# The S5 matrix to the state made row-major from transposed factors, with SyncE carrying its loads

## The chip, the core and the metric

The kernel runs on one NeuronCore of a Trainium2 chip. The core has five engines with an instruction queue each: TensorE (PE in the profile; its weight loads are PEld), VectorE (DVE), ScalarE (ACT), GpSimd (POOL) and SyncE (SP), which here only issues DMAs. The DMAs of all queues share 16 DMA engines. An engine runs its queue in order: where an instruction waits for a semaphore, all behind it wait too. The metric is the device time in microseconds.

## The reference, cut to what matters

One step of a hybrid diffusion backbone: two layers, each a SwiGLU feed-forward half, a mixer and a second feed-forward half, on 128 context and 256 latent tokens of width 1024. One branch of the mixer is a bidirectional diagonal state-space layer (S5) with 32 groups of 16 channels and 64 complex states for each direction:

```python
abar_r, abar_i = mag * jnp.cos(a_im * dt), mag * jnp.sin(a_im * dt)
...
bbar_r = qr[..., None] * b_re - qi[..., None] * b_im
bbar_i = qr[..., None] * b_im + qi[..., None] * b_re
bu_r = jnp.einsum('gph,blgh->blgp', bbar_r, u)
bu_i = jnp.einsum('gph,blgh->blgp', bbar_i, u)
...
_, _, sr, si = lax.associative_scan(_ssm_combine, (ar, ai, bu_r, bu_i), reverse=reverse, axis=1)
y = jnp.einsum('ghp,blgp->blgh', c_re, sr) - jnp.einsum('ghp,blgp->blgh', c_im, si)
```

The kernel works the scan in chunks of 8 tokens. Three tables for each group hold what a chunk needs: the *matrix to the state* (`ms`: a power of `abar` times `bbar`, for each of 8 positions and 16 channels), the *matrix from the state* (`my`: a power times `c`), and the *responses* inside a chunk (`k_d`, gathered to `mi`). They depend on weights alone.

## The kernel before

TensorE runs in an order written by hand; the orders of the other four engines come from a scheduler that places each instruction by its priority and by the time at which it reckons the operands to be there.

**Weights.** All projections stream weights in *units* of 128 x 1024 values (512 KB): SyncE loads `wr` (L149), ACT copies it to the rounded `wh` (L126), VectorE makes the rest `wl` (L105, called as `sub`), and TensorE runs `mm3`, three matmuls for each of 8 tiles of a unit: `wh` by the high half of the input (L198), `wh` by the low half (L199) and `wl` by the high half (L200). `wr`, `wh` and `wl` have three buffers each, and a unit is prepared two units ahead (`LOOK = 2`). The names in the trace are `mm<-hh,wh` and the like, by input.

**Side work.** Everything that isn't a projection is a generator, called a track; at each unit the running tracks are advanced by some steps, a step ending at a `yield`. `tables(0)` runs as a track beside the first feed-forward half of layer 0, `tables(1)` beside the first half of layer 1, both with the loads of the modulation weights (`modw` on SyncE, L374, then 8 matmuls each, L386).

**The tables.** `s5_tables(l)` (L924) goes over four blocks `gb` of 8 groups. For each block it transposes `cr` into `cT`, makes `bb` (the discretised `bbar`, states along the partitions, by `cmul`) and its spread-out copy `bp` (four ACT copies, L968 and L969), and loads the raw inputs of the next block (`load_bc`, on GpSimd's queue). Then come two sub-blocks `sb` of four groups. Each has six VectorE products and sums of 128 x 512 for `my`, six more for `mt` (the matrix to the state, states along the partitions), the matmuls of the responses (L1024, L1034), and eight transposes of `mt` on TensorE (in the helper `transpose`, L138), whose results ACT copies to `ms` (L1050, two of 128 x 512) before GpSimd's queue writes `ms` to DRAM. The powers of `abar` are expanded once in `s5_params` and read back as `pxl` tiles.

Of the kernel before, what the change touches and what calls it, by code (L numbers as in the profile page):

```python
# [11 lines left out]
F32 = mybir.dt.float32  # L12
# [44 lines left out]
def hybrid_step(ctx: ExitStack, tc: tile.TileContext, I, pos_r, pos_c, y_prompt, y_sample, new_state):  # L57
# [43 lines left out]
    def s1(shape, name):  # L101
        return sp.tile(shape, F32, tag="s1", name=name, bufs=7)
# [616 lines left out]
    px_d = [drm.tile([P, 2, 2, TC, G], F32, tag=f"px{l}", name=f"px{l}") for l in range(DEPTH)]  # L719
# [68 lines left out]
    def s5_params(raw, ldt):  # L788
# [81 lines left out]
        lo_i = slice(TC - 1, None, -1), slice(1, TC + 1)  # L870
        hi_i = slice(0, TC), slice(TC, 0, -1)
        for w in range(2):
            px = c4([P, DEPTH, 2, TC, G], "px")
            for i in range(2):
                for rows, ix in ((LO, lo_i[w]), (HI, hi_i[w])):
                    src = pw[rows, i, ix, :].rearrange("p n (l g) -> p l n g", l=DEPTH)
                    for l in range(DEPTH):
                        act.activation(px[rows, l, i], src[:, l], AF.Copy)
            for l in range(DEPTH):
                q.dma_start(px_d[l][:, w], px[:, l])  # L880
# [43 lines left out]
    def s5_tables(l):  # L924
        q = nc.gpsimd
        px = []
        for w in range(2):
            t = c2([P, 2, TC, G], "pxl")
            q.dma_start(t, px_d[l][:, w])
            px.append(t)  # L930
        psx, pyx = px
# [18 lines left out]
        for gb in range(G // GB):  # L950
# [9 lines left out]
            pool.memset(bb, 0.0)  # L960
# [5 lines left out]
            pool.memset(bp, 0.0)  # L966
# [4 lines left out]
            ts_(nci, cT[:, 1], -1.0)  # L971
            if gb + 1 < G // GB:
                nxt = load_bc(gb + 1)
            kall = s1([P, 2, 9 * H], "kall")
            for sb in range(GB // GS):
                s0 = sb * GS

                def pexp(tab, i):
                    v = tab[:, i, :, g0 + s0 : g0 + s0 + GS]
# [6 lines left out]
                b_r, b_i = vec(bb[:, 0]), vec(bb[:, 1])  # L986
                my = c4([P, GS, 2, TC, H], "my")
                t1, t2 = c2(sh, "tp1"), c2(sh, "tp2")
# [864 lines left out]
```

## Time and profile before

| | |
|---|---|
| median of 3 runs | 1775.85 us (1775.21 to 1778.99) |
| profiled execution, own time | 1775.03 us |
| its span | 1773.0 us |
| mean granted clock of TensorE | 0.997 |
| TensorE busy | 1743.7 us (98% of the span) |
| VectorE busy | 1246.8 us (70%) |
| ACT busy | 795.8 us (45%) |
| moved by DMA | 344.48 MB, mean 194 GB/s |

The profile is one execution. The busy time of an engine is summed over its instructions; matmuls overlap their neighbours, so a main matmul of 0.34 us is followed by the next after about 0.17 us. A line of a timeline gives start, duration, engine, line, operation, tiles, shapes and count, and in square brackets the idle time of the engine before it with what ended it. All VectorE products have the line of the helper, L105, so they are told apart by their tiles. The span leaves out some 2 us around it.

### The profile page before, as it was taken

The numbers are of one execution on the slowest core, as the hardware profiler recorded it, in microseconds if no ns is written. First come the engines' busy times: TensorE is split into PE (matmuls) and PEld (weight loads), VectorE is DVE, ScalarE is ACT, GpSimd is POOL, SyncE is SP. The second block draws the span as 40 slices with busy tenths as digits, with TensorE's granted clock in tenths as the row PEclk, the third lists the DMA queues.
The fourth block names the chain that finished last, engine by engine and source line by source line (L and its number), as shares of the span: only waits on it lengthen the run. The fifth ranks groups of instructions, "written<-read, shape, count | busy, mean of one in ns | idle before, by whom it ended". The sixth has DMA issues, their size and how long they took to land.

```text
span 1773.0 us, 30946 instructions
## 1 busy us (share of the span) xinstructions
PE 1743.7 (98%) x12116; PEld 1652.8 (93%) x12116; DVE 1246.8 (70%) x2344; ACT 795.8 (45%) x1330; POOL 203.5 (11%) x400
## 2 busy tenths in 40 slices
PE   7999999999999999999999999999999999999997
PEld 4899999999999989999999899999999999999997
DVE  5496676778986885678487666767799788544435
ACT  3344333575355553233366233336744546423233
POOL 2012343310010000000001133232100000000000
PEclk9999999999999999999999999999999999999999
DMA  9778788776753677788346776667666443444332
GB/s 343 249 224 275 231 252 269 226 198 190 240 157 108 186 238 228 237 280 257 112 131 208 234 224 215 175 195 233 162 210 200 131 123 116 132 130 127 123 125 77
DMA packets 253753, 344.48 MB, mean 194 GB/s; under 512 B 22399, under 2 KB 216651, under 8 KB 253608
## 3 DMA queue, kind: packets, MB, share of 16 engines
q1 hardware_dynamic: 228504, 299.18, 53.4%
q0 software_dynamic: 17088, 39.51, 7.5%
q10 hardware_dynamic: 8016, 3.82, 0.8%
q8 instruction: 95, 1.56, 0.4%
q14 instruction: 50, 0.41, 0.1%
HBM read 309.75 MB, written 32.70 MB: 193 GB/s over the span
## 4 chain that ended last, share of the span: by engine, by line
PE 81%; DVE 10%; ACT 4%; DMA 3%; issue 2%; SPq 0%; ACTq 0%; DVEq 0%
PE mm L198 25%; PE mm L200 25%; PE mm L199 25%; PE ax L386 3%; DVE wl L105 3%; DVE cacc L123 2%; DMA wr<-in_w_gate_dram 1%; DVE m_t L105 1%; PE tb L138 1%; ACT wh L126 1%; DVE m_hh L105 1%; DMA modw<-in_w_mod_dram 1%; DVE macc L123 1%; DMA wr<-in_w_in_dram 1%; ACT zp L1125 0%
## 5 line engine op out<-in xcount | busy, mean ns | idle before, releaser
L105 DVE TENSOR_TENSOR wl<-wr,wh 128x1024 fp32r<-128x1024 f32 (+2 forms) x389 | 457.0, 1175 | 352.1 <-ACT wh L126 347.4
L126 ACT ACTIVATE wh<-wr 128x1024 fp32r<-128x1024 f32 (+1 forms) x387 | 395.9, 1023 | 613.9 <-PE mm L199 443.9
L198 PE MATMUL mm<-hh,wh 128*128 128x384 f32 x1840 | 625.3, 340 | 2.7 <-ACT hh L621 2.7
L200 PE MATMUL mm<-hh,wl 128*128 128x384 f32 x1840 | 617.1, 335 | 4.4 <-DVE wl L105 4.2
L199 PE MATMUL mm<-hl,wh 128*128 128x384 f32 x1840 | 616.3, 335 | 0.5 <-DVE hl L105 0.3
L198 PEld LDWEIGHTS mm<-hh,wh 128*128 128x128 f32 x1840 | 345.9, 188 | 31.7 <-issue 18.1
L200 PEld LDWEIGHTS mm<-hh,wl 128*128 128x128 f32 x1840 | 345.8, 188 | 6.7 <-DVE wl L105 6.7
L199 PEld LDWEIGHTS mm<-hl,wh 128*128 128x128 f32 x1840 | 345.9, 188 | 1.2 <-DVE hl L105 1.1
L198 PE MATMUL mm<-ah,wh 128*128 128x384 f32 x800 | 273.2, 342 | 0.0
L199 PE MATMUL mm<-al,wh 128*128 128x384 f32 x800 | 269.4, 337 | 0.8 <-DVE al L105 0.8
L200 PE MATMUL mm<-ah,wl 128*128 128x384 f32 x800 | 270.0, 338 | 0.0
L198 PEld LDWEIGHTS mm<-ah,wh 128*128 128x128 f32 x800 | 150.2, 188 | 10.2 <-issue 6.7
L199 PEld LDWEIGHTS mm<-al,wh 128*128 128x128 f32 x800 | 150.4, 188 | 1.7 <-DVE al L105 1.1
L200 PEld LDWEIGHTS mm<-ah,wl 128*128 128x128 f32 x800 | 150.2, 188 | 0.0
L123 DVE SCALAR_TENSOR_TENSOR x<-mm,gt,x 128x128 f32<-128x128 f32 x224 | 83.1, 411 | 33.3 <-PE mm L200 33.1
L198 PE MATMUL mm<-xh,wh 128*128 128x386 f32 x240 | 84.7, 353 | 0.0
L126 ACT ACTIVATE ah<-av 128x384 fp32r<-128x384 f32 x82 | 42.1, 519 | 89.4 <-DVE av L105 89.1
L200 PE MATMUL mm<-xh,wl 128*128 128x386 f32 x240 | 81.9, 341 | 0.0
L199 PE MATMUL mm<-xl,wh 128*128 128x386 f32 x240 | 81.9, 341 | 0.0
L123 DVE SCALAR_TENSOR_TENSOR macc<-modw,silu_c,macc 128x1024 f32<-128x1024 f32 x56 | 69.9, 1278 | 14.9 <-DMA modw<-in_w_mod_dram 14.9
L123 DVE SCALAR_TENSOR_TENSOR cacc<-pad,pv,cacc 128x399 f32<-128x399 f32 x120 | 69.7, 627 | 0.0
L386 PE MATMUL ax<-modw,silu_c 128*32 128x512 f32 (+1 forms) x576 | 63.2, 511 | 0.7 <-DMA modw<-in_w_mod_dram 0.7
(316 smaller groups left out, 1820.0 us busy)
## 6 DMA issues: line engine op xcount, KB each, us to landing
wr<-in_ffn_w_dram SPq DMA_DIRECT2D x256, 512.0 KB, 3.6
modw<-in_w_mod_dram SPq DMA_DIRECT2D x144, 512.0 KB, 5.4
wr<-in_w_gate_dram SPq DMA_DIRECT2D x48, 512.0 KB, 3.8
wr<-in_w_in_dram SPq DMA_DIRECT2D x24, 512.0 KB, 3.6
my<-my POOLq DMA_DIRECT2D x16, 512.0 KB, 5.5
ms<-ms POOLq DMA_DIRECT2D x16, 512.0 KB, 4.9
m_ms<-ms SPq DMA_DIRECT2D x16, 512.0 KB
m_my<-my SPq DMA_DIRECT2D x16, 512.0 KB, 7.4
```

The lines of the kernel that those rows point to most:

```text
L105: (eng or dve).tensor_tensor(out, a, b, op=op)
L123: dve.scalar_tensor_tensor(out, a, s, b, op0=op0, op1=op1)
L126: act.activation(hi, full, AF.Copy)
L138: pe.transpose(out, in_, ident[:rows, :rows])
L198: pe.matmul(out, wh[:, k, cols], xh, start=first, stop=False)
L199: pe.matmul(out, wh[:, k, cols], xl, start=False, stop=False)
L200: pe.matmul(out, wl[:, k, cols], xh, start=False, stop=last)
L386: pe.matmul(b[32 * s : 32 * s + 32, :w], silu_c[:, k, :], raws[i][:, c : c + w], start=(k == 0), stop=(k == KD - 1), skip_group_check=True,)
```

## The change

The matrix to the state is made with the 128 chunk rows (position and channel) along the partitions, the layout in which it is needed, so that its transposes go. What is transposed instead are its factors. `s5_params` transposes the powers once (eight transposes, tile `pws`) and writes them to DRAM as `pt_d`. For each block, `factor_rows` transposes a copy `bc` of `bb` (two transposes), ACT copies the result to `bts`, and eight DMAs on GpSimd's queue write it to `btr_d`. For each sub-block `to_rows_in` loads `pt` (eight DMAs of 64 KB on SyncE, one for each position, each read 16 times over for the 16 channels) and `bt` (one of 512 KB on GpSimd's queue), and `to_rows` makes `ms` of them in six VectorE operations of 128 x 512. `load_bc` moves from GpSimd's queue to SyncE's: eight DMAs of 32 KB for each block. The fills of `bb` and `bp` move from GpSimd to VectorE, for the halves that need them, and the tag `s1` gets nine buffers in place of seven. The steps of a block are in another order: `my` of both sub-blocks first, with `factor_rows` and the responses between their steps, then `to_rows` of both.

```diff
-        return sp.tile(shape, F32, tag="s1", name=name, bufs=7)
+        return sp.tile(shape, F32, tag="s1", name=name, bufs=9)
...
+        pws = c4([P, TC, P], "pws")
+        for i in range(2):
+            b = tb_bank()
+            for m in range(TC // 2):
+                transpose(
+                    b[:, m * P : (m + 1) * P], pw[:, i, 2 * m : 2 * m + 2, :].rearrange("p n r -> p (n r)"), P
+                )
+            bv = b.rearrange("p (m s) -> p m s", s=P)
+            o = pws[:, 4 * i : 4 * i + 4]
+            act.activation(o[:, ::-1, LO], bv[:, :, LO], AF.Copy)
+            act.activation(o[:, :, HI], bv[:, :, HI], AF.Copy)
+            yield
...
-                    q.dma_start(braw[d * PS : (d + 1) * PS, i], I[nm][l, d, gs].rearrange("g p h -> p g h"))
+                    nc.sync.dma_start(braw[d * PS : (d + 1) * PS, i], I[nm][l, d, gs].rearrange("g p h -> p g h"))
...
-                    q.dma_start(cr[:, i, d, :], I[nm][l, d, gs].rearrange("g h p -> (g h) p"))
+                    nc.sync.dma_start(cr[:, i, d, :], I[nm][l, d, gs].rearrange("g h p -> (g h) p"))
...
-            pool.memset(bb, 0.0)
+            dve.memset(bb[:, :, :, H:], 0.0)
...
-            pool.memset(bp, 0.0)
+            dve.memset(bp[LO, :, :, H:], 0.0)
+            dve.memset(bp[HI, :, :, :H], 0.0)
...
+            bc = s1([P, 2, GB, H], "bc")
+            act.activation(bc, bb[:, :, :, :H], AF.Copy)
             if gb + 1 < G // GB:
                 nxt = load_bc(gb + 1)
+
+            def factor_rows():
+                b = tb_bank()
+                for i in range(2):
+                    transpose(b[:, i * P : (i + 1) * P], bc[:, i].rearrange("p g h -> p (g h)"), P)
+                bts = s1([P, 2, P], "bts")
+                act.activation(bts.rearrange("p i s -> p (i s)"), b[:, : 2 * P], AF.Copy)
+                for j in range(TC):
+                    q.dma_start(btr_d[l][j, :, gs].rearrange("h g x -> g h x"), bts.rearrange("r i s -> r (i s)"))
...
-                mt = c4([P, GS, 2, TC, H], "mt")
-                t1, t2 = c2(sh, "tp1"), c2(sh, "tp2")
-                mul(t1, pexp(psx, 0), b_r)
-                mul(t2, pexp(psx, 1), b_i)
+
+            def to_rows_in(sb):
+                gr = slice(g0 + sb * GS, g0 + (sb + 1) * GS)
+                pt = c4([P, 2, GS, P], "pt")
+                for j in range(TC):
+                    nc.sync.dma_start(pt[j * H : (j + 1) * H], pt_d[l][:, j, gr].unsqueeze(0).to_broadcast([H, 2, GS, P]))
+                bt = c4([P, GS, 2 * P], "bt")
+                q.dma_start(bt, btr_d[l].rearrange("j h g x -> (j h) g x")[:, gr])
...
+            def to_rows(sb):
+                pt, bt = ins[sb]
+                ms = c4([P, GS, 2, P], "ms")
+                t1, t2 = (c2([P, GS, P], f"tp{i}") for i in (1, 2))
+                mul(t1, pt[:, 0], bt[:, :, 0])
+                mul(t2, pt[:, 1], bt[:, :, 1])
                 yield
...
-                ms = c4([P, GS, 2, P], "ms")
-                for g2 in range(0, GS, 2):
-                    b = tb_bank()
-                    for j in range(4):
-                        transpose(
-                            b[:, j * P : (j + 1) * P], mt[:, g2 + j // 2, j % 2].rearrange("p i h -> p (i h)"), P
-                        )
-                    act.activation(ms[:, g2 : g2 + 2].rearrange("p g r c -> p (g r c)"), b, AF.Copy)
-                q.dma_start(ms_d[l][:, g0 + s0 : g0 + s0 + GS], ms)
+
+            mys, ins = [], []
+            yield
+            for n, _ in enumerate(from_rows(0)):
+                if n == 1:
+                    factor_rows()
+                yield
+            for n, _ in enumerate(from_rows(1)):
+                if n == 0:
+                    responses(0)
+                yield
+            to_rows_in(0)
+            yield
+            responses(1)
+            yield
+            to_rows_in(1)
+            yield from to_rows(0)
+            yield from to_rows(1)
```

The rows of the order below are of layer 0, around the start of the third block. The numbers behind the names are the tiles' own; the units that matter are, in the kernel after, `wr_2791`/`wl_2794`, then those of `wl_2837`, of `wr_2945` and `wr_3003`/`wl_3006`, one behind the other, and later `wr_3151`.

TensorE before, at the end of a unit in a sub-block's middle (`my_2904` and `mt_2946` are the two matrices of the sub-block):

```order
L200 MATMUL mm_3036<-hh3_373,wl_2960 128x384
L1024 MATMUL tb_3067<-my_2904,bp_2885 32x128 x8
L1034 MATMUL tb_3067<-cT_2868,bb_2873 32x16 x4
L1034 MATMUL tb_3067<-nci_2891,bb_2873 32x16 x4
L138 MATMUL tb_3086<-ident_92,mt_2946 128x128 x4
L138 MATMUL tb_3092<-ident_92,mt_2946 128x128 x4
L198 MATMUL mm_3035<-hh4_519,wh_2995 128x384
```

TensorE after, at the end of the unit `wl_2794`; `bc_2932` is the copy of `bb_2911`, with which the third block begins:

```order
L199 MATMUL mm_2833<-al_2631,wh_2793 128x384
L200 MATMUL mm_2833<-ah_2630,wl_2794 128x384
L138 MATMUL tb_2984<-ident_92,bc_2932 128x128 x2
L198 MATMUL mm_3001<-ah_1931,wh_2836 128x384
L199 MATMUL mm_3001<-al_1932,wh_2836 128x384
L200 MATMUL mm_3001<-ah_1931,wl_2837 128x384
```

The eight transposes of `mt` no longer stand between two units; two transposes of `bc` stand between others, at an earlier place of the block.

VectorE before, around the `wl` that goes before the first `mt` sum (`pxl_1471` is the expanded power):

```order
L105 TENSOR_TENSOR tp2_2911<-pxl_1473,cT_2868 128x512
L105 TENSOR_TENSOR tp1_2947<-pxl_1471,bb_2873 128x512
L123 SCALAR_TENSOR_TENSOR my_2904<-tp1_2910,tp2_2911 128x4x128
L123 SCALAR_TENSOR_TENSOR x5_106<-mm_2817,gt00_118,x5_106 128x256
L105 TENSOR_TENSOR tp2_2948<-pxl_1471,bb_2873 128x512
L105 TENSOR_TENSOR wl_2996<-wr_2993,wh_2995 128x1024
L105 TENSOR_TENSOR mt_2946<-tp1_2947,tp2_2948 128x4x128
L105 TENSOR_TENSOR tp1_2988<-pxl_1471,bb_2873 128x512
```

VectorE after, from `wl_3006`, the unit three behind `wl_2794` (`pt_2725` and `bt_2734` belong to the last sub-block of the block before):

```order
L105 TENSOR_TENSOR wl_3006<-wr_3003,wh_3005 128x1024
L105 TENSOR_TENSOR tp1_2787<-pt_2725,bt_2734 128x512
L105 TENSOR_TENSOR tp2_2788<-pt_2725,bt_2734 128x512
L105 TENSOR_TENSOR tp1_2822<-pt_2725,bt_2734 128x512
L105 TENSOR_TENSOR ms_2786<-tp1_2787,tp2_2788 128x4x128
L105 TENSOR_TENSOR tp2_2823<-pt_2725,bt_2734 128x512
L977 MEMSET bb_2911 128x16x16
L105 TENSOR_TENSOR ms_2786<-tp1_2822,tp2_2823 128x4x128
L105 TENSOR_TENSOR bb_2911<-cm1_2913,cm2_2914 128x8x16
L105 TENSOR_TENSOR bb_2911<-cm1_2918,cm2_2919 128x8x16
L983 MEMSET bp_2923 64x16x16
L984 MEMSET bp_2923 64x16x16
```

The six operations of `ms_2786` now follow `wl_3006` in one run, and `bb_2911` of the next block stands behind them.

SyncE before, over five units and two loads of modulation weights:

```order
L149 DMA wr_2957<-in_ffn_w1_dram 128x4x256
L149 DMA wr_2993<-in_ffn_w1_dram 128x4x256
L374 DMA modw_3134<-in_w_mod_dram 128x1024
L374 DMA modw_3136<-in_w_mod_dram 128x1024
L149 DMA wr_3037<-in_ffn_w1_dram 128x4x256
L149 DMA wr_3104<-in_ffn_w1_dram 128x4x256
L149 DMA wr_3155<-in_ffn_w1_dram 128x4x256
```

SyncE after, over the units from `wr_3003` to `wr_3151`:

```order
L149 DMA wr_3003<-in_ffn_w1_dram 128x4x256
L1043 DMA pt_2725<-pt0_142 16x2x512 x2
L149 DMA wr_3059<-in_ffn_w1_dram 128x4x256
L374 DMA modw_3181<-in_w_mod_dram 128x1024
L374 DMA modw_3183<-in_w_mod_dram 128x1024
L149 DMA wr_3107<-in_ffn_w1_dram 128x4x256
L1043 DMA pt_2725<-pt0_142 16x2x512 x2
L149 DMA wr_3151<-in_ffn_w1_dram 128x4x256
L1043 DMA pt_2725<-pt0_142 16x2x512 x3
```

The chunks of `pt_2725` now stand between the loads of units, the last three behind `wr_3151`, and the loads of the next block's inputs behind these.

## Rows read from the trace of the kernel before

**Rows 1.** The page, first lines: span; busy time of each engine, share, count.
```profile
span 1773.0 us, 30946 instructions
...
PE 1743.7 (98%) x12116; PEld 1652.8 (93%) x12116; DVE 1246.8 (70%) x2344; ACT 795.8 (45%) x1330; POOL 203.5 (11%) x400
```

**Rows 2.** Waits of TensorE: line, releaser, us in total, times, longest.
```profile
PE ax L138 <- DMA crow<-in_c_dram: 5.3, 1, 5.3
PE mm L200 <- DVE wl L105: 4.2, 5, 1.4
```

**Rows 3.** Windows: us, busy of PE, PEld, DVE, ACT, POOL, clock, DMA share, GB/s.
```profile
264.00:308.00 44.00, 44.00 (x323) 39.94 (x316) 29.61 (x48) 16.20 (x27) 15.70 (x31) 1.00 0.86 278
```

**Rows 4.** Timeline of TensorE, table stage: start, us, engine, line, tiles, count.
```profile
248.66 0.34 PE L199 MATMUL mm<-al,wh 128*128 128x384 f32 x1
...
250.54 0.44 PE L138 MATMUL tb<-ident,cr 128*128 128x128 f32 x2
250.73 0.42 PE L198 MATMUL mm<-ah,wh 128*128 128x384 f32 x1
```

**Rows 5.** Timeline of ACT at the same place.
```profile
249.04 1.06 ACT L126 ACTIVATE wh<-wr 128x1024 fp32r<-128x1024 f32 x1 [3.42 <-PE mm L199]
251.01 0.39 ACT L958 ACTIVATE cT<-tb 128x256 f32<-128x256 f32 x1 [0.92 <-PE tb L138]
252.33 0.31 ACT L968 ACTIVATE bp<-bb 64x128 f32<-64x128 f32 x1 [0.94 <-DVE bb L105]
```

**Rows 6.** Timeline of VectorE at the same place.
```profile
250.13 1.23 DVE L105 TENSOR_TENSOR wl<-wr,wh 128x1024 fp32r<-128x1024 f32 x1
...
252.52 0.28 DVE L105 TENSOR_TENSOR bb<-cm,cm 128x128 f32<-128x128 f32 x1
252.72 1.89 DVE L105 TENSOR_TENSOR tp<-pxl,cT 128x512 f32<-128x512 f32 x3
...
260.36 1.23 DVE L105 TENSOR_TENSOR wl<-wr,wh 128x1024 fp32r<-128x1024 f32 x1 [0.17 <-ACT wh L126]
261.50 0.68 DVE L105 TENSOR_TENSOR mt<-tp,tp 128x512 f32<-128x512 f32 x1
```

**Rows 7.** Timeline of the issues on SyncE at the same place.
```profile
250.63 0.82 SPq L374 DMA_DIRECT2D modw<-in_w_mod_dram  x2
251.58 10.41 SPq L149 DMA_DIRECT2D wr<-in_ffn_w_dram  x3
```

**Rows 8.** The chain of waits: start, us, engine, tile, line, count.
```profile
179.78 1.17 PE tb L138 x8
...
269.60 1.12 PE tb L138 x8
...
1198.59 1.17 PE tb L138 x8
```

**Rows 9.** TensorE by line and form: busy us, mean ns, idle before.
```profile
L138 PE MATMUL tb<-ident,mt 128*128 128x128 f32 x128 | 19.3, 287 | 0.0
```

**Rows 10.** Issues of DMAs: count, KB each, median us to landing.
```profile
mib<-kd POOLq DMA_DIRECT2D x64, 64.0 KB, 5.6
...
wr<-in_ffn_w_dram SPq DMA_DIRECT2D x16, 256.0 KB, 2.8
...
m_rho<-rhod SPq DMA_DIRECT2D x8, 200.0 KB, 8.6
```

**Rows 11.** Timeline of TensorE around 360 us, and a window of it.
```profile
360.61 0.37 PE L468 MATMUL ax<-ones,sqacc 128*32 128x1 f32 x24 [1.96 <-DVE sqacc L105]
...
362.26 0.53 PE L200 MATMUL mm<-xh,wl 128*128 128x386 f32 x1
...
360.00:365.00 5.00, 4.39 (x38) 4.38 (x39) 4.96 (x14) 1.54 (x3) 0.00 (x0) 0.66 0.91 305
```

**Rows 12.** Waits of SyncE: line, releaser, us in total, times, longest.
```profile
SPq L149 <- DVE wl L105: 1088.7, 322, 8.0
```

More of the change, by code (lines that the diff above doesn't have):

```diff
@@ L718, in hybrid_step @@
     rho_d = [drm.tile([P, 4, G // 4, NE], F32, tag=f"rhod{l}", name=f"rhod{l}") for l in range(DEPTH)]
-    px_d = [drm.tile([P, 2, 2, TC, G], F32, tag=f"px{l}", name=f"px{l}") for l in range(DEPTH)]
+    px_d = [drm.tile([P, 2, TC, G], F32, tag=f"px{l}", name=f"px{l}") for l in range(DEPTH)]
+    pt_d = [drm.tile([2, TC, G, P], F32, tag=f"pt{l}", name=f"pt{l}") for l in range(DEPTH)]
+    btr_d = [drm.tile([TC, H, G, 2 * P], F32, tag=f"btr{l}", name=f"btr{l}") for l in range(DEPTH)]
     NG = DEPTH * G
@@ L868, in s5_params @@
             yield
[L870 to L878, printed above, removed]
-            for l in range(DEPTH):
-                q.dma_start(px_d[l][:, w], px[:, l])
+        px = c4([P, DEPTH, 2, TC, G], "px")
+        for i in range(2):
+            for rows, ix in ((LO, slice(1, TC + 1)), (HI, slice(TC, 0, -1))):
+                src = pw[rows, i, ix, :].rearrange("p n (l g) -> p l n g", l=DEPTH)
+                for l in range(DEPTH):
+                    act.activation(px[rows, l, i], src[:, l], AF.Copy)
+        for l in range(DEPTH):
+            q.dma_start(px_d[l], px[:, l])
+        yield
[11 more added lines that the diff above has]
+            yield
+        for n2 in range(2):
+            for l in range(DEPTH):
+                r = n2 * NG + l * G
+                rows_d = pt_d[l].rearrange("i j g s -> (i j) g s")
+                for half, off in ((LO, 1 - n2), (HI, n2)):
+                    q.dma_start(
+                        rows_d[off::2, :, half].rearrange("m g s -> g m s"), pws[r : r + G, :, half]
+                    )
         yield
@@ L925, in s5_tables @@
         q = nc.gpsimd
[L926 to L931, printed above, removed]
+        pyx = c2([P, 2, TC, G], "pxl")
+        q.dma_start(pyx, px_d[l])
         def load_bc(gb):
@@ L993, in s5_tables @@
                 t1, t2 = c2(sh, "tp1"), c2(sh, "tp2")
[L994 removed]
+                mul(t1, pexp(1), c_r)
                 yield
[L996 removed]
+                mul(t2, pexp(0), c_i)
                 stt(
@@ L1006, in s5_tables, with responses @@
                 yield
-                mt = c4([P, GS, 2, TC, H], "mt")
-                t1, t2 = c2(sh, "tp1"), c2(sh, "tp2")
-                mul(t1, pexp(psx, 0), b_r)
-                mul(t2, pexp(psx, 1), b_i)
+            def to_rows_in(sb):
[5 more added lines that the diff above has]
+                q.dma_start(bt, btr_d[l].rearrange("j h g x -> (j h) g x")[:, gr])
+                bt = bt.rearrange("p g (i s) -> p g i s", s=P)
+                ins.append((pt, bt))
+            def to_rows(sb):
[4 more added lines that the diff above has]
+                mul(t2, pt[:, 1], bt[:, :, 1])
                 yield
-                sub(mt[:, :, 0], t1, t2)
-                t1, t2 = c2(sh, "tp1"), c2(sh, "tp2")
-                mul(t1, pexp(psx, 0), b_i)
+                sub(ms[:, :, 0], t1, t2)
+                t1, t2 = (c2([P, GS, P], f"tp{i}") for i in (1, 2))
+                mul(t1, pt[:, 0], bt[:, :, 1])
                 yield
-                mul(t2, pexp(psx, 1), b_r)
-                add(mt[:, :, 1], t1, t2)
-                for _ in range(3):
-                    yield
+                mul(t2, pt[:, 1], bt[:, :, 0])
+                add(ms[:, :, 1], t1, t2)
+                q.dma_start(ms_d[l][:, g0 + sb * GS : g0 + (sb + 1) * GS], ms)
+                yield
+            def responses(sb):
+                s0 = sb * GS
+                my = mys[sb]
                 b = tb_bank()
```

17 lines of the change are left out of this document (9 added, 8 removed).

## The prediction

> **What bounds the kernel now.** Read the page's first part first: TensorE is busy for 1743.7 of 1773.0 us [rows 1]. Next come the waits of TensorE: the longest single one is 5.3 us, at the start, and the low halves of the weights (`wl`) cost it 4.2 us in all [rows 2]. In the middle of the stage that the change rewrites it is busy for 44.00 of 44.00 us at a granted clock of 1.00, with the DMA engines at 0.86 [rows 3]. So a matmul taken off TensorE comes off the time almost whole, and a wait put on TensorE goes on whole: it runs in one written order, has nothing else to do, and no later slack gives it back.
>
> Then read how a weight unit passes from engine to engine; the rest rests on it. The last L199 of a unit started at 248.66 and ran 0.34 us [rows 4], so its `wh` buffer came free at 249.0 = E. ACT, which had waited 3.42 us for that, made the new `wh` in 1.06 [rows 5]; VectorE made `wl` of it in 1.23, ending at 251.36 [rows 6]; SyncE issued the next `wr` into the freed raw buffer at 251.58 [rows 7]. With three buffers each, that `wl` belongs to the unit three further on and that `wr` to the one six further on. So VectorE can't pass the `wl` of unit u+3 before E(u) + 2.3 us, nor SyncE the `wr` of u+6 before E(u) + 2.6.
>
> The kernel before lives with this because TensorE uses what lies behind such a `wl` only about two units later: the `mt` product that follows the `wl` of 260.36 ran at 261.50 [rows 6], and TensorE's transposes that need it came at 269.60 [rows 8].
>
> **The change: what leaves TensorE.** The 128 transposes of `mt` stand in the chain as 16 groups of 8, at 1.09 to 1.17 us, of which three are shown [rows 8]: 16 x 1.12 = 17.9 us. They are on the path, since TensorE stands still nowhere around them [rows 3]; their 32 evictions leave ACT, which was not the bound. By the Trainium skill ("TensorE: Matmul & The Clock Gate", Part 4: PE-mode transpose) a transpose took about 275 ns in one kernel's context, so that 128 would be an estimated 35 us; the rows have 287 ns for one as well [rows 9], but eight of them overlap into 1.12 us, and the rows decide.
>
> What comes instead: 8 pairs of factor transposes, bounded by the pair of `cr`, which moved the next main matmul by 0.19 us and lengthened it by 0.08 [rows 4], so 8 x 0.3 = 2.4; and 8 transposes of the powers, once, like one group, 1.1. Net for TensorE: 17.9 - 3.5 = **-14 us**.
>
> **The change: what now waits.** Nothing before shows the new order's waits; they follow from the three excerpts of the order. After unit `wl_2794` TensorE's very next instruction is now the transpose of `bc_2932`. That needs ACT's copies of `bb` (four to `bp`, one to `bc`), these need VectorE's two `bb` differences, and these stand on VectorE behind `wl_3006`, the unit three further on, and behind the six operations of `ms_2786`, which need all of `pt_2725`. The last three of its eight chunks stand on SyncE behind `wr_3151`, six further on. TensorE therefore waits for a relay that only its own last matmul sets off. Its price here, from E:
>
> - `wh` and `wl`: 2.3 us, as above; the `wr` can be issued at 2.6.
> - SyncE issues one `wr` and three chunks at 0.41 each (two took 0.82 [rows 7]), to 4.2; the last lands later by something not shown for this shape. Nearest are 2.8 for a weight of 256 KB and 5.6 for `mib`, 64 KB written by small rows [rows 10]; the chunks are 64 KB in rows of 2 KB, so I take 3.6, nearer the weights: 7.8. The short end is nothing (the chunk has landed by 2.3), the long one 8.6, that of the `m_rho` load [rows 10].
> - VectorE: six operations of 128x512 at 0.63 (three took 1.89 [rows 6]) = 3.8, the fill of `bb` about 0.3 (as its 0.28 subtractions, a guess from the nearest row) and two differences at 0.28 = 4.7: 12.5.
> - ACT: four copies at 0.31 and one like `cT` at 0.39 [rows 5] = 1.6: **14 us**.
>
> The same chain stands at the start of the second, third and fourth group block of both layers, with different covers (the first blocks have no `to_rows` ahead of them). In layer 0 the three places have chunks behind the `wr`: about 14.5, 14 and 14. In layer 1 the first has five chunks behind it: 14. The second's chunks stand behind an older `wr` and have landed: 2.3 + 4.7 + 1.6 = 8.6. The third has its `wl` out of the way; left are the last products, differences and copies, about 5, and 2 more for the `my` product that `responses` wants one unit later: 7. Sum: 14.5 + 14 + 14 + 14 + 8.6 + 7 = **+72 us**. With the chunks landed in time everywhere it is 4 x 8.6 + 8.6 + 7 = 50; with landings of 5.6 it is 80, with 8.6 it is 92.
>
> **The clock.** The trace has one idle TensorE of such a kind: 1.96 us before 360.61. A main matmul at 362.26 then took 0.53 us where its like take 0.34 [rows 4], and the slice 360 to 365 has a granted clock of 0.66 [rows 11], so the engine fell from 2.4 to 1.2 GHz for a part of it. (1 - 0.66) x 5 = 1.7 us lost. Six longer stalls: 6 x 1.7 = **+10 us**, from none (if the fall lies inside the stall) to twice that.
>
> **What I cost at nothing.** 24 MB more of transfers (128 chunks of 64 KB, 16 `bt` of 512 KB, 64 writes of factor rows of 128 KB) beside what fills 0.86 of the DMA engines in this stage [rows 3]: while TensorE stands, the queues drain, so they lose no weights of their own. The stage moved 278 GB/s, and 305 in the slice with the clock's fall [rows 3, 11], so there is a little room above. The eight loads of `b` and `c` a block on SyncE: 8 x 0.4 us of issue, hidden by the two units of weights ahead, but they add to the head of each queue they stand in. The fills on VectorE: 0.3 us each, on the chain at six places and counted there. The evictions of `pws` and of the factor rows go to ACT, in the place of 32 longer ones.
>
> **Sum.** The profiled execution took 1775.0 us (0.8 below the median of 1775.85, its span 2.0 below it). 1775 - 14 + 72 + 10 = **1843 us**.
>
> **Rivals.** *Hidden.* The queue a load is issued from makes no difference, and the waits fold into slack. The Trainium skill ("DMA: Bandwidth & Descriptors", Issuing engines are not separate DMA queues) says that spreading issues over engines saves only the sequencer's time, usually small; read so, gathering them on SyncE would cost next to nothing. As a mechanism here: SyncE's chunks would be out before TensorE reaches the end of the unit, and VectorE's differences too; 1775 - 14 = **1761**. It would need VectorE to run past `wl` of unit u+3 before E(u); ACT's 3.42 us of waiting for L199 [rows 5] speaks against it, and three `wr` issues that took 10.41 us [rows 7], with SyncE's 322 waits for `wl` of 1088.7 us in all [rows 12], show that what is long is the wait at the queue's head, not the issue. Chance 0.06, with 0.02 more for a case in which a single place waits and takes the 14 us back (about 1775).
> *Lump alone.* The chunks are always there in time and the clock recovers inside the stall: 1775 - 14 + 50 = **1811**, or 1797 if the two lesser places of layer 1 are hidden too. Chance 0.12.
> *Slower still.* Landings like `m_rho`'s, in a stage whose DMA engines are nearly full, and the clock's fall doubled: 1775 - 14 + 92 + 20 = **1873**. Chance 0.10 for over 1868.
> Where it turns: each place costs 8.6 us even with its chunks landed, so two places outweigh the 14 us; faster needs five of the six to be hidden.
>
> **How the numbers follow.** Forecast 0.70 (1815 to 1868, itself at 1843), lump alone 0.12 (1797 to 1815), slower still 0.10, hidden 0.06, even 0.02. The range goes from 1797 to 1873. A measurement here can tell about 0.2% (3.6 us). Faster 0.06, same 0.02, slower 0.92.
>
> **What would show it.** TensorE's waits in the new trace name ACT's `bc` (L991) at six places, 5 to 15 us each, right after a unit's last matmul and with `tb<-ident,bc` behind; ahead of it VectorE waits for a DMA of `pt`; the granted clock is down in the slices behind. `tb<-ident,mt` is gone, with pairs of `bc` in its place at about 0.3 us each. The forecast is wrong if these transposes find `bc` done, if their waits name the landing of the factor rows or of `cr` instead, or if TensorE waits for `wl` or `wr` all through the stage.

## The result and the profile after

The changed kernel takes 1851.34 us (median; 1848.57 to 1851.52) beside 1775.72 us for the kernel before on the same chip: a ratio of 1.0427, 95% interval 1.0411 to 1.0444. It is slower by 75.6 us. The forecast was 1843 us, slower, with a range of 1797 to 1873; its mechanism is the one that the trace shows.

The page and the waits of TensorE in the kernel after answer [rows 1] and [rows 2]. First the page (span; busy time of each engine, its share, its instructions):

```profile
span 1846.8 us, 31022 instructions
...
PE 1740.1 (94%) x12012; PEld 1648.8 (89%) x12012; DVE 1252.9 (68%) x2368; ACT 783.2 (42%) x1310; POOL 206.0 (11%) x404
```

The waits of TensorE (line, releaser, us in total, times, longest):

```profile
PE tb L138 <- ACT bc L991: 72.5, 6, 17.3
...
PE ax L138 <- ACT modev L396: 3.3, 3, 1.5
PE mm L200 <- DVE wl L105: 3.1, 7, 1.4
...
PE tb L1072 <- DVE my L123: 1.3, 1, 1.3
```

TensorE's busy time is 3.6 us less, the span 73.8 us more, and one line that did not exist before holds 72.5 us: the factor transposes wait for ACT's `bc`, six times. The six, in the timeline of TensorE (start, duration, line, tiles, shapes, and in brackets the idle time before with its releaser):

```profile
233.96 0.69 PE L138 MATMUL tb<-ident,bc 128*128 128x128 f32 x2 [17.30 <-ACT bc L991]
...
288.59 0.69 PE L138 MATMUL tb<-ident,bc 128*128 128x128 f32 x2 [13.87 <-ACT bc L991]
...
349.88 0.47 PE L138 MATMUL tb<-ident,bc 128*128 128x128 f32 x1 [15.02 <-ACT bc L991]
...
1116.31 0.47 PE L138 MATMUL tb<-ident,bc 128*128 128x128 f32 x1 [16.99 <-ACT bc L991]
...
1174.19 0.48 PE L138 MATMUL tb<-ident,bc 128*128 128x128 f32 x1 [8.21 <-ACT bc L991]
...
1224.83 0.44 PE L138 MATMUL tb<-ident,bc 128*128 128x128 f32 x2 [1.15 <-ACT bc L991]
```

They are the second, third and fourth block of each layer. The second row is the place whose order the excerpts show; its relay can be read engine by engine, as [rows 5 to 7] do for the place before. ACT:

```profile
274.58 1.06 ACT L126 ACTIVATE wh<-wr 128x1024 fp32r<-128x1024 f32 x1 [3.64 <-PE mm L199]
286.83 0.31 ACT L986 ACTIVATE bp<-bb 64x128 f32<-64x128 f32 x1 [11.19 <-DVE bb L105]
...
288.12 0.42 ACT L991 ACTIVATE bc<-bb 128x256 f32<-128x256 f32 x1
```

VectorE:

```profile
275.67 1.23 DVE L105 TENSOR_TENSOR wl<-wr,wh 128x1024 fp32r<-128x1024 f32 x1 [0.17 <-ACT wh L126]
282.62 1.90 DVE L105 TENSOR_TENSOR tp<-pt,bt 128x512 f32<-128x512 f32 x3 [5.73 <-DMA braw<-in_s_b_im_dram]
...
286.46 0.48 DVE L105 TENSOR_TENSOR bb<-cm,cm 128x128 f32<-128x128 f32 x2
```

The issues on SyncE:

```profile
271.92 1.77 SPq L1043 DMA_DIRECT2D pt<-pt  x2
276.92 0.40 SPq L149 DMA_DIRECT2D wr<-in_ffn_w_dram  x1
277.36 1.44 SPq L1043 DMA_DIRECT2D pt<-pt  x3
278.90 1.28 SPq L955 DMA_DIRECT2D braw<-in_s_b_re_dram  x2
```

TensorE's last L199 of the unit frees `wh` at 274.6. `wh` and `wl` end at 276.9, the `wr` goes out at 276.92, the three last chunks of `pt` end their issue at 278.8, VectorE starts the six operations at 282.62, its `bb` ends at 286.9, ACT's `bc` at 288.5, and TensorE goes on at 288.59: 14.0 us after it had set the relay off. That VectorE's releaser is named as a load of `b` and not as `pt` is taken up in the second experiment.

### The profile page after: what moved, and what is told of

The parts are those of the page before. It is cut to its first block, busy times and chain, and to the rows that moved or that the text cites. A ratio compares the mean times of both kernels' runs of the same rounds, so it can differ in the third digit from the quotient of the medians.

```text
span 1846.8 us, 31022 instructions
## 1 busy us (share of the span) xinstructions
PE 1740.1 (94%) x12012; PEld 1648.8 (89%) x12012; DVE 1252.9 (68%) x2368; ACT 783.2 (42%) x1310; POOL 206.0 (11%) x404
## 4 chain that ended last, share of the span: by engine, by line
PE 79%; DVE 12%; DMA 3%; issue 3%; ACT 2%; SPq 1%; DVEq 0%; ACTq 0%
PE mm L198 25%; PE mm L199 24%; PE mm L200 24%; PE ax L386 3%; DVE wl L105 3%; DVE cacc L123 2%; DVE tp L105 1%; DVE m_t L105 1%; DVE m_hh L105 1%; DMA wr<-in_w_gate_dram 1%; DMA pt<-pt 1%; ACT wh L126 1%; DVE macc L123 1%; DMA wr<-in_w_in_dram 1%; DMA wr<-in_ffn_w_dram 1%
## 5 line engine op out<-in xcount | busy, mean ns | idle before, releaser
L199 PE MATMUL mm<-hl,wh 128*128 128x384 f32 x1840 | 619.1, 336 | 0.7 <-DVE hl L105 0.7
L199 PEld LDWEIGHTS mm<-hl,wh 128*128 128x128 f32 x1840 | 348.5, 189 | 1.5 <-DVE hl L105 1.4
L198 PE MATMUL mm<-ah,wh 128*128 128x384 f32 x800 | 274.6, 343 | 0.0
L199 PE MATMUL mm<-al,wh 128*128 128x384 f32 x800 | 270.5, 338 | 1.3 <-DVE al L105 1.3
L199 PEld LDWEIGHTS mm<-al,wh 128*128 128x128 f32 x800 | 151.0, 189 | 2.8 <-DVE al L105 2.3
L199 PE MATMUL mm<-xl,wh 128*128 128x386 f32 x240 | 81.4, 339 | 0.0
L123 DVE SCALAR_TENSOR_TENSOR macc<-modw,silu_c,macc 128x1024 f32<-128x1024 f32 x56 | 69.9, 1276 | 14.5 <-DMA modw<-in_w_mod_dram 14.5
L138 PE MATMUL tb<-ident,bc 128*128 128x128 f32 x16 | 4.7, 388 | 72.5 <-ACT bc L991 72.5
L138 PEld LDWEIGHTS tb<-ident,bc 128*128 128x128 f32 x16 | 2.1, 180 | 76.5 <-ACT bc L991 75.6
```

Of the source, the lines that this page charges most:

```text
L123: dve.scalar_tensor_tensor(out, a, s, b, op0=op0, op1=op1)
L138: pe.transpose(out, in_, ident[:rows, :rows])
L198: pe.matmul(out, wh[:, k, cols], xh, start=first, stop=False)
L199: pe.matmul(out, wh[:, k, cols], xl, start=False, stop=False)
```

## The experiments

The theory is the relay: TensorE asks for a thing that stands on VectorE (and its load on SyncE) behind work that only the end of TensorE's own last unit releases. The *distance* of a place is how many units further on VectorE has the thing than TensorE wants it: the number of the last `wl` ahead of it on VectorE, less that of the unit that TensorE has just ended. In the kernel after it is 3 at five of the six places and 1 at the last; a count in the traces gives the same as the orders. The *lump* is the run of `to_rows` operations that stands on VectorE ahead of the thing. The rivals: SyncE's queue as such, the 24 MB more of transfers, the loads of `b` and `c`, the copy to `bc`.

### The chunks back on GpSimd's queue

```diff
-                    nc.sync.dma_start(pt[j * H : (j + 1) * H], pt_d[l][:, j, gr].unsqueeze(0).to_broadcast([H, 2, GS, P]))
+                    q.dma_start(pt[j * H : (j + 1) * H], pt_d[l][:, j, gr].unsqueeze(0).to_broadcast([H, 2, GS, P]))
```

> The kernel after, with the pt chunks alone back on GpSimd's queue. In its order VectorE's bb differences stand behind the wl of the unit 2, 3 and 3 further on than the one after which TensorE wants bc (blocks two to four of layer 0) and 1, 3 and 2 further in layer 1; in the kernel after it was 3, 3, 3, 3, 3, 1. Relay theory: what decides is that distance, not the queue; at 3 the wait is 2.3 us for wh and wl, twice 3.8 us for both to_rows that now stand there, and 2.5 us for the differences and copies = 12 us; at 1 or 2 it is under 5. Three places of 12, three of 3 and 6 us of clock: 1775 - 14 + 36 + 9 + 6 = 1812, range 1795 to 1830. Rival, that SyncE's queue is the cause: with no chunk behind a wr the waits for bc vanish, 1761 to 1770.

Measured: 1832.8 us, ratio 1.0321 (1.0304 to 1.0338). The waits of TensorE in it:

```profile
PE tb L138 <- ACT bc L991: 31.1, 5, 9.2
PE ax L138 <- ACT modev L396: 12.0, 4, 5.3
```

The three places with a distance of 3 waited 9.2, 8.8 and 9.2 us, the others 3.1 us or less. So SyncE's queue is not the cause by itself: without a chunk behind a `wr`, and with VectorE waiting for `pt` no longer than 2.5 us anywhere, 57 us are still lost, and the waits for `bc` go with the distance. The order changed with the queue, so the run does not tell what the queue alone is worth. The time is 20 us over the expectation and outside its range: the waits for `bc` came out below the 45 us of its sum, but it lacked the new waits for `modev` (12.0 in place of 3.3) and for `my` (7.3), and the rest stays open.

### The loads of b and c back on GpSimd's queue

```diff
-                    nc.sync.dma_start(braw[d * PS : (d + 1) * PS, i], I[nm][l, d, gs].rearrange("g p h -> p g h"))
+                    q.dma_start(braw[d * PS : (d + 1) * PS, i], I[nm][l, d, gs].rearrange("g p h -> p g h"))
...
-                    nc.sync.dma_start(cr[:, i, d, :], I[nm][l, d, gs].rearrange("g h p -> (g h) p"))
+                    q.dma_start(cr[:, i, d, :], I[nm][l, d, gs].rearrange("g h p -> (g h) p"))
```

> The kernel after, with the eight loads of b and c per block alone back on GpSimd's queue; pt stays on SyncE. The distances are as in the kernel after. In the trace after, VectorE's wait ahead of the second to_rows is put down at two places to the landing of a load of b (13.3 us in two waits), which stands behind the last pt chunk on the same queue. Relay theory: that name is a neighbour of the true one, the last pt chunk, and nothing changes: waits for bc 68 to 76 us in all, time 1843 to 1855. Rival, that the loads of b hold VectorE: waits for bc fall by 8 us or more, time under 1842.

Measured: 1860.4 us, ratio 1.0468 (1.0441 to 1.0494); TensorE waits 80.8 us for `bc`. VectorE's waits in it:

```profile
DVE tp L105 <- DMA pt<-pt: 47.1, 9, 11.3
```

At the two places where the trace after names a load of `b` (5.7 and 7.6 us), the same operation now waits for `pt` by name, for 9.2 and 6.8 us, with the loads of `b` gone from the queue. So the loads of `b` and `c` on SyncE are not what holds VectorE; that the name in the trace after was that of a neighbour of the last chunk is the reading that fits. The time came out some 9 us longer than after, outside the expected range; 8.3 of it stand in the waits for `bc`. Why the chunks hold VectorE longer here is not shown.

### The loads of b and c on SyncE in the kernel before

```diff
-                    q.dma_start(braw[d * PS : (d + 1) * PS, i], I[nm][l, d, gs].rearrange("g p h -> p g h"))
+                    nc.sync.dma_start(braw[d * PS : (d + 1) * PS, i], I[nm][l, d, gs].rearrange("g p h -> p g h"))
...
-                    q.dma_start(cr[:, i, d, :], I[nm][l, d, gs].rearrange("g h p -> (g h) p"))
+                    nc.sync.dma_start(cr[:, i, d, :], I[nm][l, d, gs].rearrange("g h p -> (g h) p"))
```

> The kernel before, with only the eight loads of b and c of each block moved from GpSimd's queue to SyncE's. Relay theory: there is no chunk and no relay there, the loads have a block's time to land, and SyncE has two units ahead: 1772 to 1779, no change. Rival, that loads on SyncE's queue hold up the weights behind them: 8 issues of 0.4 to 0.6 us for each of 8 blocks, up to 30 us, 1780 or more with TensorE waiting for wl.

Measured: 1773.2 us, ratio 0.999 (0.9978 to 1.0002): no change. In the kernel before, this part of the change is free, as the prediction had it.

### bb and bc of the next block made ahead of to_rows

`prep(gb)` holds what the block began with: `cT`, `bb`, `bp`, `nci`, `bc` and the loads for the block behind it.

```diff
             responses(1)
+            if gb + 1 < G // GB:
+                tabs = prep(gb + 1)
             yield
             to_rows_in(1)
```

> The kernel after, with cT, bb, bp and bc of the next block made before the two to_rows of a block instead of behind them. VectorE's bb then stands 2 or 3 units ahead of the point at which TensorE wants bc, so no wait there. But my of the first sub-block stays behind both to_rows: 3 units further on than its use at five places, and 2 at one. Relay theory: the wait moves from bc to my, with the same wl, the same chunk landing and to_rows, and four of the six operations of my in place of the copies: 5 places of about 14 and one of 3, time 1840 to 1855, TensorE's waits naming my and not bc. Rival, that the copies bb to bc are the bottleneck: the waits go, 1761 to 1775.

Measured: 1877.4 us, ratio 1.0576 (1.0557 to 1.0596). The waits of TensorE:

```profile
PE tb L1079 <- DVE my L105: 90.0, 5, 21.5
```

No wait for `bc` is left, and the wait moved to the next thing behind the same products, `my`, at the five places that the distances named, 15.4 to 21.5 us each. It is dearer than expected (14 each), and the time is 22 us above the expected range. Making one operand early does not help while the next one stands behind the same lump.

### One DMA for pt

```diff
-    pt_d = [drm.tile([2, TC, G, P], F32, tag=f"pt{l}", name=f"pt{l}") for l in range(DEPTH)]
+    pt_d = [drm.tile([TC, G, 2, P], F32, tag=f"pt{l}", name=f"pt{l}") for l in range(DEPTH)]
...
-                for j in range(TC):
-                    nc.sync.dma_start(pt[j * H : (j + 1) * H], pt_d[l][:, j, gr].unsqueeze(0).to_broadcast([H, 2, GS, P]))
+                nc.sync.dma_start(
+                    pt,
+                    pt_d[l].rearrange("j g i s -> j g (i s)")[:, gr].rearrange("j g x -> j (g x)").unsqueeze(1).to_broadcast([TC, H, GS * 2 * P]),
+                )
```

> The kernel after, with the powers in DRAM as (position, group, part, state), so that pt of a sub-block is one DMA of 512 KB on SyncE in place of eight of 64 KB. The bytes and the queue are as after. In its order the bb differences stand only 1 or 2 units further on than TensorE's use (1, 2, 2, 1, 1, 1) and my 2 at the most. Relay theory: at a distance of 2 the wl can pass one unit earlier (4.3 us), so waits of 0 to 5 us at each place, 12 us in all, clock 2: 1775 - 14 + 14 = 1775, range 1763 to 1785. Rivals: that the 24 MB more, or SyncE's queue as such, hold the kernel: 1830 or more as before.

Measured: 1832.7 us, ratio 1.0322 (1.0291 to 1.0353): the expectation of 1775 was wrong. The waits of TensorE and of VectorE in it:

```profile
PE mm L200 <- DVE wl L105: 31.4, 15, 7.8
PE mm L198 <- DVE x L123: 10.2, 2, 9.5
```

```profile
DVE tp L105 <- DMA bt<-btr: 91.3, 7, 17.5
```

The waits for `bc` are gone (1.2 us), as the distances said. But the scheduler now puts a block's first `to_rows` earlier, 4 to 6 units behind the factor transposes in place of 7 to 12, and its other operand, `bt`, has not landed: it comes through ACT, eight writes, and a read behind them on GpSimd's queue. VectorE stands still at the head of its queue, with `wl`, `x` and `al` behind it, and TensorE runs out of weights. The relay was replaced by another.

### Everything used later

On top of the one DMA for `pt`: the factor rows are written once and `bt` reads them eight times over, `prep` runs ahead of `to_rows` as above, and the steps stand in another order. `done()` is the gathering of `mib` of the block before.

```diff
-                for j in range(TC):
-                    q.dma_start(btr_d[l][j, :, gs].rearrange("h g x -> g h x"), bts.rearrange("r i s -> r (i s)"))
+                q.dma_start(btr_d[l][:, gs].rearrange("h g x -> g h x"), bts.rearrange("r i s -> r (i s)"))
...
+            if gb:
+                factor_rows()
             yield
             for n, _ in enumerate(from_rows(0)):
-                if n == 1:
+                if gb == 0 and n == 2:
                     factor_rows()
                 yield
-            for n, _ in enumerate(from_rows(1)):
-                if n == 0:
-                    responses(0)
+            yield from from_rows(1)
+            if gb == 0:
+                yield
                 yield
             to_rows_in(0)
             yield
-            responses(1)
+            responses(0)
             yield
             to_rows_in(1)
+            if gb:
+                done()
+            yield
+            responses(1)
+            if gb + 1 < G // GB:
+                tabs = prep(gb + 1)
+            yield
             yield from to_rows(0)
             yield from to_rows(1)
```

> The new method in another order. pt is one DMA of 512 KB for each sub-block on SyncE; the factor rows are written once (one DMA of 128 KB) and read eight times over (one DMA); bb, bp and bc of the next block are made ahead of the two to_rows; the factor transposes come first in a block, both responses after my, to_rows two steps later, and the gathering of mib waits until the next block's bt is issued. In its order bb stands 1 to 3 units ahead of TensorE's use (one place 1 behind), my 2 to 5 ahead, and to_rows 7 to 10 units behind the factor transposes that feed it (5 to 6 in the run with one pt DMA, where VectorE waited 91.3 us for bt). Relay theory: no wait of TensorE for bc, my or wl over 2 us, so only the transposes saved: 1775 - 14 = 1761, range 1757 to 1769. Rivals: more bytes hold the weights, or the six row-major operations on VectorE are dearer: 1775 or more.

Measured: 1817.7 us, ratio 1.0231 (1.0213 to 1.0249). The expectation of 1761 was wrong again, and for the same operand. VectorE's waits, then those of GpSimd's queue:

```profile
DVE tp L105 <- DMA bt<-btr: 101.0, 9, 16.7
```

```profile
POOL bt L1056 <- PE tb L1095: 85.5, 7, 21.9
```

No wait for `bc` or `my` is left on TensorE. The second line says why `bt` is late here: with the responses later, the buffers of `my`, of which `bt` takes one, come free only after TensorE has run them. Nor was `to_rows` later on VectorE: the trace has a block's first one 4 or 5 units behind the factor transposes, not the 7 to 10 of the expectation.

### The rows meant to have time to land

Added to the last run: the write of the factor rows on ACT's queue, `bt` read on SyncE beside `pt`, the responses right behind `my`, six idle steps ahead of `to_rows`, and the tables started at 2 and 3 units in place of 8.

```diff
-                q.dma_start(btr_d[l][:, gs].rearrange("h g x -> g h x"), bts.rearrange("r i s -> r (i s)"))
+                nc.scalar.dma_start(btr_d[l][:, gs].rearrange("h g x -> g h x"), bts.rearrange("r i s -> r (i s)"))
...
-                q.dma_start(
+                nc.sync.dma_start(
                     bt, btr_d[l][:, gr].rearrange("h g x -> h (g x)").unsqueeze(0).to_broadcast([TC, H, GS * 2 * P])
                 )
...
             to_rows_in(1)
...
+            for _ in range(6):
+                yield
```

> As the run with everything used later, but each piece of the row-major path now has time to land: the one write of the factor rows goes on ACT's queue, right behind the copy that makes them, bt is read on SyncE beside pt, the responses follow my so that its buffers come free for pt and bt before these are wanted, the two to_rows come six steps after the loads are issued, and the tables start earlier (2 and 3 units in place of 8) to make room. In the run before, VectorE's waits for bt were 101.0 us in 9, and TensorE's for wl behind them 34.5. Relay theory: with bt landed, VectorE doesn't wait at to_rows (under 10 us in all), TensorE's waits in the two stages fall under 8 us, and the time is 1775 - 14 to 1775 - 6: 1761 to 1769. Rival, that the stage has no room for 16 MB more beside the weights: TensorE still waits for wl by 15 us or more with bt landed in time, time over 1775.

Measured: 1816.4 us, ratio 1.0217 (1.0194 to 1.0239); 1761 to 1769 was expected. VectorE still waits for `bt`, 74.8 us in 9, and now ACT waits 134.3 us in 33 for the weights of the feed-forward halves to land, where it was 9.7 in 3 in the kernel before. At the worst place: the issue on SyncE, VectorE and ACT, and the DMA engines meanwhile (the last but one and the last column are their share and GB/s):

```profile
293.29 0.60 SPq L1056 DMA_DIRECT2D bt<-btr  x1
```

```profile
313.00 1.29 DVE L105 TENSOR_TENSOR tp<-pt,bt 128x512 f32<-128x512 f32 x2 [13.47 <-DMA bt<-btr]
```

```profile
308.31 1.06 ACT L126 ACTIVATE wh<-wr 128x1024 fp32r<-128x1024 f32 x1 [10.10 <-DMA wr<-in_ffn_w_dram]
```

```profile
296.00:300.00 4.00, 4.00 (x25) 4.00 (x24) 3.50 (x10) 1.66 (x5) 0.00 (x0) 1.00 1.07 217
300.00:304.00 4.00, 4.00 (x25) 4.00 (x24) 0.00 (x0) 0.00 (x0) 0.57 (x1) 1.00 1.10 183
304.00:308.00 4.00, 2.33 (x16) 1.17 (x14) 0.00 (x0) 0.00 (x0) 0.00 (x0) 1.00 1.05 262
```

`bt` was issued at 293.29, VectorE came to it at 299.53, and it was released at 313.00, 19.7 us after the issue. From 296 to 308 the DMA engines are full, at 183 to 262 GB/s. The rows did not get the time that was meant for them, though: at five of the nine waits VectorE was there less than 5 us after the issue of `bt`, or ahead of it. And the reads were slow: from issue to release the nine took 7.5 to 19.7 us. The rival had `bt` landed in time and no room for the weights beside it. The first did not come about, so this run can't show the second by itself; the next runs tell how much goes with the reads. That `bt` reads each row eight times over here may add to its time; no run tells that apart.

### The reads left out

In the kernel after (first run) and in the run above (second), `pt` is loaded once for a layer and that tile stands for `pt` and `bt` of every sub-block.

```diff
+                if not held:
+                    pt = c4([P, 2, GS, P], "pt")
...
+                    held.append((pt, pt.rearrange("p i g s -> p g i s")))
+                ins.append(held[0])
...
-                ins.append((pt, bt))
```

> The kernel after, leaving out the reading of its factors: pt is loaded once for a layer (eight chunks), and that tile stands for pt and for bt of every sub-block, so the matrix to the state has wrong values. All else stays: factor transposes, writes of the factor rows, six row-major operations for each sub-block, the loads of b and c on SyncE, 16 MB less moved. Its order puts bb 1 or 2 units further on than TensorE's use. If the reads alone (their landing, and where the scheduler puts work because of it) make the waits: waits of TensorE in the two stages under 15 us, 1761 to 1772. Rival, that the rest of the method costs by itself: 1780 or more.

> The same left out of the run whose tables start earlier and whose to_rows come six steps after the loads (values wrong again). There bb stands 4 to 7 units ahead of its use and nothing is waited for by VectorE at to_rows. If the reads are what was left in that run (74.8 us of VectorE's waits for bt, 1816 us): 1757 to 1767, the transposes' saving whole. Rival, that the order itself costs: 1775 or more.

Measured: 1780.1 us, ratio 1.0022 (1.0011 to 1.0033), and 1768.2 us, ratio 0.9953 (0.9938 to 0.9967). Both came out above their ranges, the first by 8 us, right at the rival's edge, the second by 1. The first still has two places of the relay, both with a distance of 2:

```profile
PE tb L138 <- ACT bc L992: 15.1, 2, 8.2
```

They are 6.9 and 8.2 us long, near the 8.6 of the relay without a landing. Two more places of this run have a distance of 2 as well, and TensorE does not wait there: at 2 the distance alone does not decide. Without the reads 71 of the 75.6 us go in the kernel after; in the later order, which was 39.6 us over the kernel before, 47 go, which leaves a gain of 7.7, and ACT's waits for the weights fall from 134.3 to 13.0 us. The waits thus hang on the reads: on their landing, and on where the scheduler puts work because of them. Leaving the reads out changed the order of the first too (distances of 1 and 2 in place of 3), so the two shares are not told apart here.

### The stalls filled

```diff
             def factor_rows():
+                fill = FILL[l][gb - 1] if gb else 0
+                x = state["x"]
+                for k in range(0, fill, 8):
+                    w = tb_bank()
+                    for _ in range(min(8, fill - k)):
+                        pe.matmul(w[:, :NT], x[:, :P], x[:, :NT], start=True, stop=True)
                 b = tb_bank()
```

> The kernel after, with useless matmuls on TensorE (128x384, 0.173 us each, into a spare bank) ahead of the factor transposes at the five places with long waits: 94, 74 and 81 in layer 0, 92 and 41 in layer 1, that is 16.3, 12.8, 14.0, 15.9 and 7.1 us, each about 1 us less than the wait measured there. The waits themselves stay, only TensorE isn't idle in them. Theory of the clock: the fall to 1.2 GHz behind each stall costs 10 us in all; with the engine busy the granted clock stays at 1.00 and the kernel, with more work, takes 1841 (1836 to 1845) against 1851. Rival: the fall lies inside the stalls and costs nothing: 1851, or a few us more where a fill is too long.

Measured: 1842.7 us, within the expected range, ratio 1.0375 (1.0357 to 1.0393), beside 1.0427 (1.0411 to 1.0444) for the kernel after: some 8.6 us faster by the medians (3 to 15 by the ends of the two intervals) with 382 matmuls more. The wait that is left:

```profile
PE tb L138 <- ACT bc L993: 10.0, 6, 2.7
```

The mean granted clock of the run is 0.995 (0.977 after, 0.997 before). So the fall of the clock behind the stalls costs time, 8.6 us or somewhat more (the 382 matmuls at 0.173 us and the waits that are left add up to 66 + 10 us, 3.6 over the waits after).

### The transposes alone

```diff
-                    b = tb_bank()
-                    for j in range(4):
-                        transpose(
-                            b[:, j * P : (j + 1) * P], mt[:, g2 + j // 2, j % 2].rearrange("p i h -> p (i h)"), P
-                        )
-                    act.activation(ms[:, g2 : g2 + 2].rearrange("p g r c -> p (g r c)"), b, AF.Copy)
+                    act.activation(
+                        ms[:, g2 : g2 + 2].rearrange("p g r c -> p (g r c)"),
+                        mt[:, g2 : g2 + 2].rearrange("p g r i h -> p (g r i h)"),
+                        AF.Copy,
+                    )
```

> The kernel before, leaving out the 128 transposes of mt alone: ACT copies mt to ms as it stands (same size of copy, values in the wrong places, so the S5 branch is not computed rightly). It measures what the removed work is worth with nothing put in its place. By the chain of waits 16 groups of 1.12 us: 1775.4 - 17.9 = 1757.5, range 1755 to 1761. Rival, that a part of the groups hides other waits: 1765 or more. By 287 ns for each transpose, if they didn't overlap: 1739.

Measured: 1760.5 us, ratio 0.991 (0.9895 to 0.9925): the 128 transposes are worth 15.2 us, 13 to 19 by the interval, so little or nothing hides them.

## Why the prediction was right, and where its terms were off

**The bound and what leaves TensorE.** The prediction took the 128 transposes at 17.9 us by the chain of waits [rows 8]; with them taken out alone the kernel gained 15.2 (13 to 19). What came instead it took at 3.5. In the trace after, the pairs and the eight of the powers stand as (busy time, mean ns)

```profile
L138 PE MATMUL tb<-ident,bc 128*128 128x128 f32 x16 | 4.7, 388 | 72.5 <-ACT bc L991 72.5
...
L138 PE MATMUL tb<-ident,pw 128*128 128x128 f32 x8 | 1.0, 272 | 0.0
```

The busy times add up to 5.7 us, matmuls that overlap their neighbours, so 3.5 on the path is near, though not measured by itself. Net it is about -12 in place of -14 (-10 to -15 by the interval).

**What waits.** The sum of the six places was +72; they measured 72.5, with 1.3 for `my` behind the last one. Place by place: 14.5, 14 and 14 in layer 0 against 17.3, 13.9 and 15.0; 14, 8.6 and 7 in layer 1 against 17.0, 8.2 and 2.5 with the `my`. That the sum came out within 2 us is luck: the two first places were taken too short by 3 us each and the last too long by 4.5. The second place is right step by step: 2.3 for `wh` and `wl` (2.3), the last chunk landed 7.8 us behind (8.0), VectorE done at 12.5 (12.4), ACT at 14.1 (14.0). The first is short because six chunks, not three, stand behind its `wr` and the two loads of `modw`; they were issued at 0.67 us each and the last landed 5.2 us later, with the DMA engines full:

```profile
218.76 4.00 SPq L1043 DMA_DIRECT2D pt<-pt  x6
```

```profile
228.00 1.89 DVE L105 TENSOR_TENSOR tp<-pt,bt 128x512 f32<-128x512 f32 x3 [9.10 <-DMA pt<-pt]
```

```profile
222.00:227.00 5.00, 0.00 (x0) 0.00 (x0) 0.00 (x0) 0.00 (x0) 0.00 (x0) 0.50 1.00 306
```

The prediction gave that place 14.5 without a count of its own; with six chunks its own steps make 15.4. In layer 1 the first place is of the same kind: five chunks, the last landing 4.5 us behind its issue in place of 3.6; there the prediction counted the five, but its steps make 15, not the 14 that it wrote. The last place was over-sized: at its distance of 1 TensorE waited 1.15 us for `bc` and 1.3 for `my`, where 5 and 2 had been counted.

**The clock.** +10 was forecast from one idle stretch of 1.96 us [rows 11]. Behind the stall of the second place the windows show the clock column (third from the right) at 0.50 to 290 and at 0.70 to 295:

```profile
285.00:290.00 5.00, 1.41 (x5) 1.41 (x6) 4.89 (x13) 2.03 (x6) 3.16 (x6) 0.50 0.51 158
290.00:295.00 5.00, 5.00 (x22) 4.93 (x21) 4.96 (x9) 0.00 (x0) 4.58 (x9) 0.70 0.73 175
295.00:300.00 5.00, 5.00 (x58) 4.79 (x56) 1.98 (x4) 1.24 (x2) 2.49 (x5) 1.00 0.80 219
```

From 288.59, where TensorE goes on, that is 0.5 x 1.4 + 0.3 x 5 = 2.2 us lost at one stall, five times 11. The filled stalls gave back 8.6. The term of 10 lies between the two; it had 1.7 for six places, and the sixth hardly stalled.

**The sum.** 72.5 + 1.3 - 12 + 8.6 = 70, of 75.6 measured between the medians and 73.5 between the two profiled executions (1848.57 and 1775.03). The traces bear the terms out: TensorE's busy time fell by 3.6 us, near -12 + 8.6, and its idle time grew by 77.4 (106.7 for 29.3), of which 73.8 are the waits for `bc` and `my`. The rest is small waits: `modev` 3.3 for 0.5, `hh` 5.0 for 2.7. Nothing was forecast for them. The longer waits for `modev` go with the relay: they stand at 3.3 to 12.0 us in the kernel after and in the four of its variants whose lump holds TensorE at five places or more, and at 0.5 in all other runs. Those for `hh` do not: they were 4.0 with the transposes alone left out.

**What was costed at nothing.** The loads of `b` and `c` on SyncE are free in the kernel before, as measured. The 24 MB more were put down as harmless while TensorE stands, with "a little room above". In the kernel after, that held: ACT's wait for the weights of the feed-forward halves stayed at 9.7 us. In the orders without the relay it did not: ACT waited 62.8 us for them with one DMA for `pt`, 71.9 with everything used later, 134.3 with the rows meant to land. The rivals of the prediction came out as follows. *Hidden* needed five of six places covered; one was. The queue is not neutral here, since its head waits for VectorE: the three chunks cost 1.4 us of issue, but the queue had stood for 3.2 us (273.7 to 276.92) at the `wr` ahead of them, which went out when `wl` was done. By the rule in the Trainium skill ("DMA: Bandwidth & Descriptors", Issuing engines are not separate DMA queues) spreading issues over engines saves only the time of issue. The trace does not agree for an engine whose queue also carries loads that wait. *Lump alone* is what the run with the chunks on GpSimd and the first one without reads come near to: 6.9 to 9.2 us for a place that waits, 8.6 by the prediction. Its lower figure of 1797, the bottom of the range, is a slip: 1775 - 14 + 4 x 8.6 makes 1795.

## What to carry to other kernels

Where one engine runs in a fixed order and feeds the release of buffers to the others, ask of each thing that it wants how many units further on the maker's queue has to be before it gets to it; here a distance of three units cost 8 to 22 us at a place, of two nothing to 8, of one nothing to 2.4. Making one operand earlier moved the wait to the next operand behind the same lump, and one DMA in place of eight changed the order so that VectorE waited for another load instead. So all that stands behind the lump, and the order that a change leads to, have to be counted before a part is moved. Work saved on the bound engine (15 us) is a small prize beside one such wait at each of a few places, and operands that go through DRAM bring a landing that the scheduler's order may take for shorter than it is.

## What the runs showed of the hardware that was not expected

The DMA engines stood at a share of 1.05 to 1.10 at 183 to 262 GB/s in the run with the rows meant to land, and at 1.00 with 306 GB/s in the kernel after: full engines do not mean one rate. In that stretch a read of 512 KB took 19.7 us from issue to use, where `bt` landed in a median of 6.1 us in the kernel after, there with each row read once. And five stalls filled with useless matmuls made the kernel faster by some 8.6 us than the same stalls left idle.
